# Two projections of a hybrid layer as a 2x2x2 block product with seven instead of eight multiplications

## The chip, the cores and the metric

The kernel runs on one core of one Trainium2 chip. The metric is the device time of one execution in microseconds (us). The engines are named as in the profile: PE (TensorE, matrix products), DVE (VectorE), ACT (ScalarE), POOL (GpSimd) and SP (SyncE, which only issues transfers). SBUF is the on-chip memory, PSUM the accumulators of PE.

## The reference

One layer over 512 tokens of width 1024, all in float32. Only the first part matters here:

```python
proj = rmsnorm(h, norm_mix_g) @ w_in     # (512, 1024) @ (1024, 3592)
fq, fk, fv, ff, gq, gf, gi, gg = split(proj)   # 512, 512, 512, 8, 512, 512, 512, 512 columns
fox_out = fox_attention(fq, fk, fv, log_sigmoid(ff + bias))   # 8 heads of 64
rec = hgrn2_chunkwise(gq, gf, gi, lb)          # 4 heads, state 128x128, gated linear recurrence
rec = rmsnorm(rec, hgrn_norm_g) * silu(gg)
h = h + concat(fox_out, rec) @ w_out
...
```

Cross-attention to 256 memory rows, an MLP of width 4096 with a squared ReLU, and a last RMSNorm follow. `gi` are the recurrence's values, `gg` its output gates: 512 columns each, next to each other in `w_in` (2568 to 3079 and 3080 to 3591).

## The kernel before

Every float32 product is made of three matmuls on numbers of a shorter format: a matrix is split into a high part (`wh...`, by ACT, L179) and the rest (`wl...`, by DVE, L183), and hi x hi, hi x lo and lo x hi are added up in PSUM. The raw weights arrive in tiles `wr...`, loaded by SP (L205); there are two such buffers, so a load waits until the split of the tile two loads earlier has been made. The normalised tokens stand, feature-major, as `hn_hi` and `hn_lo`.

Weights come as panels, listed in `specs`, in two units `a` and `b`; the number in a tile's name is the panel's place in that list. `next_panel` takes the next panel and starts the load and the split of the one after it. Panels 0 to 3 are the recurrence's keys and queries (of `f` and `q`). Panel 4 has the first 256 columns of the values and the 8 forget columns (`proj_if`). Panels 5 and 6 are the gates (`gg`) as two halves of the contraction, 512 columns wide, and panels 7 and 8 the other 256 columns of the values and 256 of the attention's (`gi`): both are `wide` products, made by `gemm_wide` (L281 to L283) in four PSUM tiles, one for each 128 tokens. Panels 9 and up are the attention's.

The products of panels 4 to 8 are not run in one piece. They are generators in the queue `fill`, and the recurrence's preparation takes a budget of them between its own steps, so that PE has work while DVE, ACT and POOL do the elementwise part. That preparation goes through seven levels, m = 1, 2, 4 ... 64: small products `lv` on PE (L800), a masked copy into `Ac` on DVE (L806), multiplications of queries and keys (`sta`, `mov`) by the decays `F` on DVE (L825) and on DVE and POOL (L826), products of decays on POOL (L828), and copies for the next level on ACT (L777, L778). Then come the transposes `pa` of the level result (L878), the transposed keys `pk` (L917) copied to `kt` (L920, for the first block of tokens on DVE), and the scan over four blocks of 128 tokens: outputs `po` (L934), the state product `pst` from `iv` and `kt` (L940), the state, and the gated output `rec` (L961). In the scan, too, matmuls of the queue stand between the blocks.

Two more things have a clock of their own. `COPIES` says how many of the weight copies for the MLP (`wsu`, `wsd`, memory to memory, 512 KB each, issued by SP at L434) follow each weight load from which panel on. `PACE` says at which sum of matmul time and in what steps POOL's accumulating transfers for the MLP are issued.

The tokens' transposes from PSUM also go unscaled into a tile `xT`, from where POOL writes them to memory for later use (`x_park`).

Of the kernel before, what the change touches and what calls it, by code (L numbers as in the profile page):

```python
# [9 lines left out]
F32 = mybir.dt.float32  # L10
# [6 lines left out]
P = 128  # L17
# [21 lines left out]
NEG = -3.0e38  # L39
SEVEN = (1, 2, 3, 4, 5, 6, 7)  # L40
RAWS, HB, LOADS = 5, 4, 8
COPIES = {7: 2, 16: 1, 17: 0, 21: 1}
PACE = (183.0, 4.7), (306.0, 11.5)


@with_exitstack
def emit(
# [58 lines left out]
    def t4(name):  # L106
        return t4p.tile([P, D], F32, tag="t4", name=name)
# [21 lines left out]
    def f(a):  # L129
        return a.bitcast(F32)  # L130
# [58 lines left out]
    def load_unit(name, spec, ks, parts=1, between=None):  # L189

        nw = max(sl.stop for sl, _ in spec)
        uk = ks.stop - ks.start
        hi, lo = new_parts([uk, nw], name)
        state["halves"] += 1
        if len(stream) >= LATE and state["halves"] % 3 == 0:
            raw_ = t4(f"wr{name}")
        else:
            raw_ = wrp.tile([P, uk * nw], F32, tag="wr", name=f"wr{name}", padded_shape=[P, UK * UW])
        raw_ = raw_.rearrange("p (k n) -> p k n", k=uk)
        nk = uk // parts  # L200
        splits = []
        for q in range(parts):
            qs, src_ks = slice(q * nk, (q + 1) * nk), slice(ks.start + q * nk, ks.start + (q + 1) * nk)
            for sl, src in spec:
                nc.sync.dma_start(raw_[:, qs, sl], src[:, src_ks, :])  # L205
            if between is not None:
                between(q)
            for _ in range(next((n for at, n in reversed(COPIES.items()) if len(stream) >= at), 0)):
                if copies:
                    tc.keep_in_program_order(copies.popleft()())  # L210
            splits.append(split_of(hi[:, qs, :], lo[:, qs, :], raw_[:, qs, :]))
        return (hi, lo), splits

    def load_next(parts=2, between=None):

        i = len(stream)
        if i >= len(specs):
            return []
        units, splits = [], []
# [7 lines left out]
        return splits  # L227

    def next_panel():
# [178 lines left out]
    gp.affine_select(out=tri[:, 0, :], in_=tri[:, 0, :], compare_op=ALU.is_ge, fill=0.0, base=0, pattern=[[1, P]], channel_multiplier=-1)  # L408


    hn_hi, hn_lo = act_tile("hn_hi"), act_tile("hn_lo")
    xTd = drp.tile([4, P, 2, S], F32, name="xTd")

# [73 lines left out]
    park = {}  # L487

    ms0 = sm(NT, "ms0")
    gv = cp.tile([P, 33], F32, name="gv")  # L490
# [14 lines left out]
        ve.scalar_tensor_tensor(hn_lo[:, c, :], xps[c], g_mix[:, c : c + 1], f(hn_hi[:, c, :]), op0=ALU.mult, op1=ALU.subtract)  # L505

    def x_park(c):
        part, new_ = c // 2, c // 2 not in park
        if new_:
            park[part] = s4([2, S], f"xT{part}")  # L510
        dst = park[part][:, c % 2, :]
# [4 lines left out]
        if not new_:  # L516
            gp.dma_start(xTd[part], park[part])

    def x_sq(tb):
        junk = s4([D], f"x0j{tb}")  # L520
# [8 lines left out]
    with tc.manual_schedule(engines={mybir.EngineType.Activation, mybir.EngineType.DVE}):  # L529
# [121 lines left out]
    g_x, g_mem, g_ff, g_h = gv[:, 0:8], gv[:, 8:16], gv[:, 16:24], gv[:, 24:25]  # L651
    gate(3)
    forget(3)
    for hp in range(2):
        wt = next_panel()
        for j in range(2):
            h = 2 * hp + j
            ps = mm(f"gq{h}")
            run_now(gemm_fm(ps, wt, j * P, hn_hi, hn_lo))
            ve.tensor_tensor(qt_(h), ps, rbc, ALU.mult)  # L660
            ac.activation(qt_(h), qt_(h), AF.Silu)
# [26 lines left out]
    z = sm(32, "z")  # L688
    z3 = z.rearrange("p (t h) -> p t h", h=FH)

    def proj_if():
        wt = next_panel()
        for tb in range(NT):
            ps = mm(f"gi0{tb}", (WT + FH,))
            yield from gemm_tm(ps, wt, hn_hi, hn_lo, tb)
            ac.activation(iv[tb // 2][:, tb % 2, 0:WT], ps[:, 0:WT], AF.Identity, scale=r0[:, tb : tb + 1])
            ve.scalar_tensor_tensor(z3[:, tb, :], ps[:, WT : WT + FH], r0[:, tb : tb + 1], fb, op0=ALU.mult, op1=ALU.add)
# [6 lines left out]
    fill.add(proj_if(), "ff")  # L704
    fill.add(new(gg, "gg"))
    fill.add(proj_wide([lambda tb: gg[tb // 2][:, tb % 2, :]], AF.Silu, "gg"), "gg")
# [6 lines left out]
    def proj_iv():  # L713
        yield from proj_wide([lambda tb: iv[tb // 2][:, tb % 2, WT:S], new_fv()], AF.Identity, "gi")

    fill.add(proj_iv(), "iv")

# [181 lines left out]
    load_mem(0)  # L899


    mx_hi, mx_lo = act_tile("mx_hi"), act_tile("mx_lo")
    St = None
    pending = None

# [1013 lines left out]
```

## Time and profile before

| | |
|---|---|
| median of 3 runs | 751.66 us (751.61 to 752.14) |
| profiled execution | 751.99 us, of which the span is 750.3 us |
| granted clock of PE, mean | 0.998 of full speed |
| busy: PE, DVE, ACT, POOL | 742.9, 546.5, 444.7, 202.1 us |
| first level product `lv` to first `po` | 65.4 to 125.1 us |

A row of the timeline gives start and duration in us, the engine, the line, the operation, output and inputs by name, the shape, and in brackets how long the engine had been idle before and what ended that. An engine's bracket names the last release only. PE's matmuls overlap, so a matmul's duration is longer than the distance to the next. The stage that the change touches lies between about 25 and 130 us.

### The profile page before, as it was taken

To read this page: it belongs to the slowest core of one execution; us is meant where nothing else is said; L and a number is where in the kernel's file an instruction comes from. 1 tells how busy PE (TensorE), PEld (TensorE's weight loads), DVE (VectorE), ACT (ScalarE), POOL (GpSimd) and SP (SyncE) were. 2 spreads that over 40 slices of the span, in tenths; PEclk is the share of its full clock that TensorE was granted. 3 is DMA by queue.
4 is the path that set the end of the run, shared out by engine and by line. 5 is a ranking of instruction groups with operands and counts; after the bars stand their busy time and mean duration, and the time that the engine had idled before them with its cause. 6 is when DMAs were issued, how large, how long until landed. Compare 5 with 4: busy or idle time off the path is not lost.

```text
span 750.3 us, 12293 instructions
## 1 busy us (share of the span) xinstructions
PE 742.9 (99%) x4581; PEld 649.6 (87%) x4581; DVE 546.5 (73%) x869; ACT 444.7 (59%) x749; POOL 202.1 (27%) x280
## 2 busy tenths in 40 slices
PE   9999999999999999999999999999999999999996
PEld 6889888888888888888888899898989899999985
DVE  5647873667878856645556898978787887878796
ACT  5655555556666742344434589666566757574864
POOL 7207531233433237621111212111111111100034
PEclk9999999999999999999999999999999999999999
DMA  8641987578957889985579799898989898978452
GB/s 250 200 116 58 298 262 228 172 231 269 289 187 224 265 225 210 193 165 122 121 165 197 114 250 238 237 226 247 230 218 235 220 247 214 240 198 232 133 113 113
DMA packets 109678, 152.92 MB, mean 204 GB/s; under 512 B 6145, under 2 KB 76074, under 8 KB 109618
## 3 DMA queue, kind: packets, MB, share of 16 engines
q1 hardware_dynamic: 85458, 112.52, 46.3%
q0 software_dynamic: 24000, 39.35, 30.1%
q8 instruction: 36, 0.59, 0.3%
q14 instruction: 24, 0.20, 0.1%
q10 hardware_dynamic: 160, 0.27, 0.1%
HBM read 147.91 MB, written 51.40 MB: 266 GB/s over the span
## 4 chain that ended last, share of the span: by engine, by line
PE 96%; DVE 1%; issue 1%; ACT 0%; POOL 0%; POOLq 0%; DVEq 0%
PE uU L1494 4%; PE uU L1496 4%; PE uU L1495 4%; PE U L1652 3%; PE U L1653 3%; PE U L1654 3%; PE uY L1495 2%; PE uY L1494 2%; PE uY L1496 2%; PE xk L1008 2%; PE xq L253 2%; PE wo L253 2%; PE xq L254 2%; PE xq L255 2%; PE xw L255 2%; PE xw L254 2%
## 5 line engine op out<-in xcount | busy, mean ns | idle before, releaser
L183 DVE TENSOR_TENSOR wlu<-wru,whu 128x1024 fp32r<-128x1024 f32 x53 | 64.2, 1225 | 28.0 <-ACT whu L179 27.9
L179 ACT ACTIVATE whu<-wru 128x1024 fp32r<-128x1024 f32 x53 | 55.9, 1058 | 43.7 <-PE U L1654 16.8
L183 DVE TENSOR_TENSOR wld<-wrd,whd 128x1024 fp32r<-128x1024 f32 x56 | 68.3, 1222 | 13.5 <-ACT whd L179 13.2
L179 ACT ACTIVATE whd<-wrd 128x1024 fp32r<-128x1024 f32 x56 | 59.0, 1053 | 12.6 <-PE uU L1495 5.2
L1652 PE MATMUL U<-whd,hb 128*128 128x512 f32 x120 | 46.8, 390 | 0.0
L1653 PE MATMUL U<-wld,hb 128*128 128x512 f32 x120 | 46.8, 390 | 0.0
L1654 PE MATMUL U<-whd,hb 128*128 128x512 f32 x120 | 46.7, 389 | 0.0
L1029 POOL TENSOR_SCALAR bi<-nF,Ft 128x128 f32<-128x128 f32 (+3 forms) x32 | 20.6, 652 | 59.8 <-PE pt L1065 38.8
L1494 PE MATMUL uU<-xs_hi,whu 128*128 128x256 f32 x128 | 36.3, 284 | 0.0
L1496 PE MATMUL uU<-xs_hi,wlu 128*128 128x256 f32 x128 | 36.2, 283 | 0.0
L1495 PE MATMUL uY<-xs_lo,whu 128*128 128x256 f32 x128 | 36.2, 283 | 0.0
L1494 PE MATMUL uY<-xs_hi,whu 128*128 128x256 f32 x128 | 36.2, 283 | 0.0
L1496 PE MATMUL uU<-x_hi,wlu 128*128 128x256 f32 x128 | 36.2, 283 | 0.0
L1496 PE MATMUL uY<-xs_hi,wlu 128*128 128x256 f32 x128 | 36.2, 283 | 0.0
L1495 PE MATMUL uU<-xs_lo,whu 128*128 128x256 f32 x128 | 36.2, 283 | 0.0
L1495 PE MATMUL uU<-x_lo,whu 128*128 128x256 f32 x128 | 36.2, 283 | 0.0
L1494 PE MATMUL uU<-x_hi,whu 128*128 128x256 f32 x128 | 36.2, 283 | 0.0
L444 POOL DMA_DIRECT2D wsd<-in_w_dram x16 | 17.9, 1116 | 63.6 <-PE xw L255 12.8
L1390 POOL DMA_DIRECT2D wrd<-in_w_dram x8 | 9.8, 1221 | 86.2 <-DVE wld L183 85.0
L444 POOL DMA_DIRECT2D wsu<-in_w_dram x14 | 17.1, 1218 | 48.9 <-PE xw L255 15.6
L1654 PEld LDWEIGHTS U<-whd,hb 128*128 128x128 f32 x120 | 22.5, 188 | 4.7
L1652 PEld LDWEIGHTS U<-whd,hb 128*128 128x128 f32 x120 | 22.6, 188 | 4.5
(944 smaller groups left out, 2605.2 us busy)
## 6 DMA issues: line engine op xcount, KB each, us to landing
wru<-in_w_dram SPq DMA_DIRECT2D x25, 512.0 KB, 7.9
wsd<-in_w_dram SPq DMA_DIRECT2D x24, 512.0 KB, 7.3
wrd<-in_w_dram SPq DMA_DIRECT2D x24, 512.0 KB, 4.3
wrd<-wsd SPq DMA_DIRECT2D x24, 512.0 KB, 4.9
wsu<-in_w_dram SPq DMA_DIRECT2D x21, 512.0 KB, 5.6
wru<-wsu SPq DMA_DIRECT2D x21, 512.0 KB, 6.1
wsd<-in_w_dram POOLq DMA_DIRECT2D x16, 512.0 KB, 7.8
wsu<-in_w_dram POOLq DMA_DIRECT2D x14, 512.0 KB, 6.9
```

Source lines behind the costliest of these rows:

```text
L179: at = ac.activation(hi, raw, AF.Copy)
L183: at_lo = ve.tensor_tensor(lo, raw, f(hi), ALU.subtract)
L253: te.matmul(ps, wh, hi, start=n_ == 0 and not begun, stop=False)
L254: te.matmul(ps, wh, lo, start=False, stop=False)
L255: at = te.matmul(ps, wl, hi, start=False, stop=k == order[-1])
L444: yield gp.dma_start(wsum[kind, g, name], src, accum_op=ALU.add, **more)
L1494: te.matmul(ps[:, i, :], whi[:, k, ws], xh[:, k, :], start=begin, stop=False, skip_group_check=True)
L1495: te.matmul(ps[:, i, :], whi[:, k, ws], xl[:, k, :], start=False, stop=False, skip_group_check=True)
L1496: at = te.matmul(ps[:, i, :], wlo[:, k, ws], xh[:, k, :], start=False, stop=k == UK - 1, skip_group_check=True)
L1652: te.matmul(ps, hi, whi[:, k, :], start=begin, stop=False, skip_group_check=True)
L1653: te.matmul(ps, hi, wlo[:, k, :], start=False, stop=False, skip_group_check=True)
L1654: at = te.matmul(ps, lo, whi[:, k, :], start=False, stop=k == 1, skip_group_check=True)
```

## The change

Panel 4 now has the attention's 256 columns with the 8 forget columns (`proj_ff`). Values and gates together are a product of 512 tokens x 1024 with 1024 x 1024. Both factors are cut in two by two, tokens into halves of 256, contraction and columns into halves of 512, and the product is made with seven multiplications of sums of blocks instead of eight of blocks (`seven`). Each multiplication is 256 tokens x 512 x 512: 2 x 4 x 3 matmuls 128x512. They run in the order 1, 5, 6, 3, 7, 2, 4, as panels 5 to 11, and accumulate in two pairs of PSUM tiles, `gU` (1, then 6, 7 and 4 on top of it) and `gW` (5, then 3 on top of it; then 2 anew). Products 1 and 4 go to the values through ACT, 5 and 6 to the gates as plain copies on ACT. Products 2, 3 and 7 are added to what is there on DVE (L805, L813), and the gates then get their SiLU on ACT. The panels of the attention move up by three numbers: what was `wr9a` is `wr12a`.

The weight blocks 00, 01, 11 and 10 are loaded once each. 01 and 11 are loaded early, ahead of panel 4's use, into tiles that are free then; 00 goes into the two `wr` buffers; 10 replaces 11 when product 3 has been split. Sums of blocks: 01 + 11 (product 7) on POOL into four tiles, and 00 + 01 (5), that + 11 (6), and that + 10 (4) on DVE in place (L271).

The sums of token blocks are made from the tile `park`, where the unscaled transposes now stay: eight scalings on ACT, four sums on DVE, and their high and low parts on ACT and DVE into the tile `mx`, which is used for something else only later.

`COPIES` moves up with the panel numbers, and eight of the copies that followed the loads of panels 7 and 8 are now issued in two groups of four, right after block 10. `PACE` begins 5 us of matmul time earlier.

```diff
-COPIES = {7: 2, 16: 1, 17: 0, 21: 1}
-PACE = (183.0, 4.7), (306.0, 11.5)
+COPIES = {12: 2, 19: 1, 20: 0, 24: 1}
+PACE = (178.0, 4.7), (301.0, 11.5)
...
-    for n0 in (2056, 2312, 1544, 1800, 2568):
+    for n0 in (2056, 2312, 1544, 1800, 1024):
         specs.append(panel(w_in, n0))
-    specs += wide(w_in, 3080)
-    specs += wide(w_in, 2824, 1024)
+    GORDER = ("1", "5", "6", "3", "7", "2", "4")
...
+    specs += [lambda name=name: product_unit(name) for name in GORDER]
...
+    def early_blocks():
+        load_block("01", "01", [s4p.tile([P, 2, S], F32, tag="s4", name=f"wr01{u}") for u in "ab"])
+        t = t4("wr11b").rearrange("p (k n) -> p k n", k=2)
+        load_block("11", "11", [s4p.tile([P, 2, S], F32, tag="s4", name="wr11a"), t])
+        for k in range(4):
+            t = q2p.tile([P, S], F32, tag="q2", name=f"wr7{k}")
+            a, b = (raw0[n][k // 2][:, k % 2, :] for n in ("01", "11"))
+            gp.tensor_tensor(t, a, b, op=ALU.add)
+            sums7.append(t)
+
+    def product_unit(name):
+        parts = [new_parts([2, S], f"{len(stream)}{u}") for u in "ab"]
...
+            dst, a, b = {"1": (X, X, None), "5": (Y, X, Y), "6": (X, Y, Z), "3": (Z, Z, None), "2": (Z, Z, None), "4": (X, X, Z)}[name]
+            if b is not None:
+                jobs.append(lambda d=dst[u], a=a[u], b=b[u]: ve.tensor_tensor(d, a, b, ALU.add))
+            jobs.append(split_of(hi, lo, dst[u]))
+        if name == "3":
+            jobs.append(lambda: load_block("11", "10", Z))
+        if name in "37":
+            for _ in range(4):
+                jobs.append(lambda: tc.keep_in_program_order(copies.popleft()()))
+        return jobs
...
+        ve.tensor_tensor(hdif["5"], A2b, A2a, ALU.subtract)
+        ve.tensor_tensor(hdif["6"], hdif["5"], A1a, ALU.add)
+        ve.tensor_tensor(hdif["3"], hdif["6"], A1b, ALU.subtract)
+        ve.tensor_tensor(hdif["7"], A1a, A2a, ALU.subtract)
...
+            pss = U if name in "1674" else W
+            whi, wlo = next_panel()
+            xh, xl = hsum[name]
+            for u in range(2):
+                for t, ps in enumerate(pss):
...
+                        at = te.matmul(ps, lo, whi[u][:, kk, :], start=False, stop=end, skip_group_check=True)
+                        yield presum.tick(3 * S / 2400, at)
+                    if u == 1:
+                        done(name, t, ps)
+
+    fill.add(proj_ff(), "ff")
+    fill.add(new(gg, "gg"))
+    fill.add(seven(GORDER[:5]), "gg")
+    fill.add(seven(GORDER[5:]), "iv")
```

Where it moves instructions, three places matter. On PE, ahead of the scan's first block, this stood before; `gi` are products of the last panel of values, `po` and `pst` the scan's first output and state product:

```order
L917 MATMUL pk_1403<-ident,mov_462 128x128
...
L281 MATMUL gi_1170<-wh8b,hn_hi 128x512
L282 MATMUL gi_1170<-wl8b,hn_hi 128x512
L283 MATMUL gi_1170<-wh8b,hn_lo 128x512
L934 MATMUL po_1431<-iv_653,A_1288 128x128 x2
L934 MATMUL po_1431<-iv_653,A_1300 128x128 x2
L940 MATMUL pst_1436<-iv_653,kt_1408 128x128 x4
```

Now, at the same place, with `pq` the attention's first projection (panel 12):

```order
L304 MATMUL pq_1463<-hn_hi,wh12a 128x512
L305 MATMUL pq_1463<-hn_lo,wh12a 128x512
L306 MATMUL pq_1463<-hn_hi,wl12a 128x512
L304 MATMUL pq_1463<-hn_hi,wh12b 128x512
L305 MATMUL pq_1463<-hn_lo,wh12b 128x512
L306 MATMUL pq_1463<-hn_hi,wl12b 128x512
L1057 MATMUL po_1505<-iv_694,A_1355 128x128 x2
L1057 MATMUL po_1505<-iv_694,A_1367 128x128 x2
L1063 MATMUL pst_1510<-iv_694,kt_1497 128x128 x4
```

Between the transposes `pa` and `po` 15 matmuls of the attention's projection now stand, where the last products of the values stood. From the last level to `po` there are 48 matmuls instead of 57.

On DVE, around the copy `kt` that the first `pst` reads, before:

```order
L825 TENSOR_TENSOR mov_462<-mov_462,F_461 128x4x64
L183 TENSOR_TENSOR wl9b<-wr9b,wh9b 128x1024
L183 TENSOR_TENSOR wl10a<-wr10a,wh10a 128x1024
L920 COPY kt_1408<-pk_1403 128x512
L385 TENSOR_TENSOR m0m<-m0m 128x1
```

and now, with `iv` the values to which product 2 is added:

```order
L949 TENSOR_TENSOR mov_460<-mov_460,F_459 128x4x64
L805 SCALAR_TENSOR_TENSOR iv_694<-gW_990,r_432,iv_694 128x512
L805 SCALAR_TENSOR_TENSOR iv_694<-gW_991,r_432,iv_694 128x512
L188 TENSOR_TENSOR wl12a<-wr12a,wh12a 128x1024
L188 TENSOR_TENSOR wl12b<-wr12b,wh12b 128x1024
L188 TENSOR_TENSOR wl13a<-wr13a,wh13a 128x1024
L1043 COPY kt_1497<-pk_1492 128x512
```

Between the last level and `kt` there were two splits; now there are two additions and three splits. What was `wl9a` and stood ahead of the last level is now `wl12a`, behind it.

On SP, the loads of the panels behind the values (`wr`) with the copies (`wsu`, `wsd`), before:

```order
L205 DMA wr9a<-in_w_in_dram 128x4x128 x2
L434 DMA wsu_200<-in_w_dram 512x1x256
L434 DMA wsd_203<-in_w_dram 256x1x512
L205 DMA wr9b<-in_w_in_dram 128x4x128 x2
L434 DMA wsu_201<-in_w_dram 512x1x256
L434 DMA wsd_204<-in_w_dram 256x1x512
L205 DMA wr10a<-in_w_in_dram 128x4x128 x2
```

and now, from block 10 on:

```order
L243 DMA wr11a<-in_w_in_dram 128x2x512
L243 DMA wr11b<-in_w_in_dram 128x2x512
L487 DMA wsu_194<-in_w_dram 512x1x256
...
L487 DMA wsd_203<-in_w_dram 256x1x512
L210 DMA wr12a<-in_w_in_dram 128x4x128 x2
L487 DMA wsu_201<-in_w_dram 512x1x256
L487 DMA wsd_204<-in_w_dram 256x1x512
L210 DMA wr12b<-in_w_in_dram 128x4x128 x2
L487 DMA wsu_202<-in_w_dram 512x1x256
L487 DMA wsd_205<-in_w_dram 256x1x512
L210 DMA wr13a<-in_w_in_dram 128x4x128 x2
```

Eight copies stand together ahead of `wr12a`; from there on the row is as it was.

More of the change, by code (lines that the diff above doesn't have):

```diff
@@ L218, in load_next @@
             return []
+        if callable(specs[i]):
+            return specs[i]()
         units, splits = [], []
@@ L486, in emit @@
     presum.jobs.extend(j for _, j in sets)
-    park = {}
     ms0 = sm(NT, "ms0")
@@ L507, in x_park @@
     def x_park(c):
[L508 to L511, printed above, removed]
+        part, dst = c // 2, park[:, c, :]
         if c % 2 == 0:
@@ L515, in x_park @@
             ve.tensor_copy(dst, xps[c])
-        if not new_:
-            gp.dma_start(xTd[part], park[part])
+        parked.add(c)
+        if c ^ 1 in parked:
+            gp.dma_start(xTd[part], park[:, 2 * part : 2 * part + 2, :])
     def x_sq(tb):
@@ L689, in emit, with proj_ff @@
     z3 = z.rearrange("p (t h) -> p t h", h=FH)
-    def proj_if():
+    def proj_ff():
         wt = next_panel()
+        dst = new_fv()
         for tb in range(NT):
@@ L702, in new @@
         yield
-    fill.add(proj_if(), "ff")
-    fill.add(new(gg, "gg"))
-    fill.add(proj_wide([lambda tb: gg[tb // 2][:, tb % 2, :]], AF.Silu, "gg"), "gg")
     def new_fv():
@@ L711, in new_fv, with seven, tok, done @@
         return lambda tb, n0=0: t[:, tb, :]
-    def proj_iv():
-        yield from proj_wide([lambda tb: iv[tb // 2][:, tb % 2, WT:S], new_fv()], AF.Identity, "gi")
-    fill.add(proj_iv(), "iv")
+    U, W = [], []
+    def seven(names):
+        def tok(ts, tb):
+            return ts[tb // 2][:, tb % 2, :]
+        def done(name, t, ps):
+            if name == "1":
+                ac.activation(tok(iv, t), ps, AF.Identity, scale=r0[:, t : t + 1])
+            elif name == "2":
+                ve.scalar_tensor_tensor(tok(iv, t), ps, r0[:, t : t + 1], tok(iv, t), op0=ALU.mult, op1=ALU.add)
+            elif name == "4":
+                ac.activation(tok(iv, 2 + t), ps, AF.Identity, scale=r0[:, 2 + t : 3 + t])
+            elif name in "56":
+                ac.activation(tok(gg, t + (2 if name == "5" else 0)), ps, AF.Copy)
+            else:
+                tb = t + (2 if name == "7" else 0)
+                g_ = tok(gg, tb)
+                ve.tensor_tensor(g_, ps, g_, ALU.add)
+                ac.activation(g_, g_, AF.Silu, scale=nr0[:, tb : tb + 1])
+        for name in names:
+            if name == "1":
+                U.extend(mm(f"gU{t}") for t in range(2))
+            elif name == "5":
+                W.extend((mm("gW0"), pvt("gW1")))
+            pss = U if name in "1674" else W
+            whi, wlo = next_panel()
+            xh, xl = hsum[name]
+            for u in range(2):
+                for t, ps in enumerate(pss):
+                    ts_ = slice(t * P, (t + 1) * P)
+                    for kk in range(2):
+                        k = 2 * u + kk
+                        hi, lo, begin, end = xh[:, k, ts_], xl[:, k, ts_], name in "125" and k == 0, k == 3
+                        te.matmul(ps, hi, whi[u][:, kk, :], start=begin, stop=False, skip_group_check=True)
+                        te.matmul(ps, hi, wlo[u][:, kk, :], start=False, stop=False, skip_group_check=True)
+                        at = te.matmul(ps, lo, whi[u][:, kk, :], start=False, stop=end, skip_group_check=True)
[6 more added lines that the diff above has]
+    fill.add(seven(GORDER[5:]), "iv")
     Ac = []
```

54 lines of the change are left out of this document (51 added, 3 removed).

## The prediction

> **What bounds the kernel now.** The page comes first: the engines' busy shares, and the chain of work that ended last.
>
> ```profile
> PE 742.9 (99%) x4581; PEld 649.6 (87%) x4581; DVE 546.5 (73%) x869; ACT 444.7 (59%) x749; POOL 202.1 (27%) x280
> ...
> PE 96%; DVE 1%; issue 1%; ACT 0%; POOL 0%; POOLq 0%; DVEq 0%
> ```
>
> TensorE (PE) is never idle for long, and 96% of the chain is its own work. A matmul taken away is worth its full price, as long as nothing makes PE wait for its operands. So I need the price of a matmul, and who is near to being late in the stage that changes, which the windows show:
>
> ```profile
> 77.33 0.39 PE L282 MATMUL gg<-wl5a,hn_hi 128*128 128x512 f32 x1
> ...
> 78.47 0.39 PE L281 MATMUL gg<-wh5b,hn_hi 128*128 128x512 f32 x1
> ```
> ```profile
> 20.00:40.00 20.00, 20.00 (x93) 16.38 (x92) 13.72 (x23) 14.00 (x22) 3.98 (x6) 1.00 0.57 178
> 40.00:60.00 20.00, 20.00 (x129) 16.97 (x128) 9.68 (x11) 9.33 (x12) 3.51 (x2) 1.00 0.50 135
> 60.00:80.00 20.00, 20.00 (x202) 17.60 (x203) 15.70 (x33) 12.28 (x27) 12.94 (x14) 1.00 0.31 95
> 80.00:100.00 20.00, 20.00 (x168) 16.39 (x169) 14.52 (x37) 11.91 (x23) 10.33 (x14) 1.00 0.93 303
> 100.00:120.00 20.00, 20.00 (x133) 16.94 (x132) 11.64 (x22) 7.99 (x12) 4.89 (x10) 1.00 0.80 245
> ```
>
> Five matmuls after 77.33 the next one starts at 78.47, so one costs 0.228 us of PE, though each is shown 0.39 long. In the windows the columns are the stretch, its length, then busy time of PE, PEld, DVE, ACT and POOL, the granted clock (1.00: nothing to gain there) and the DMA share. DVE (VectorE) has 4.3, 5.5 and 8.4 us free in the three stretches from 60 to 120: these 18.2 us are the room for what the change adds.
>
> **The change part by part.** *The matmuls.* Values and gates took 2 x 4 x 8 x 3 = 192 matmuls 128x512; seven products of 2 x 4 x 3 are 168. 24 x 0.228 = 5.47 us less PE. Nothing is added on PE. This is the whole gain, and the rest is what PE has to wait.
>
> *The early part.* Eight scalings, four token sums and their parts fall at 30 to 55 us, where DVE and ACT are each idle 6 us of one stretch of 20 and 10 of the next. GpSimd's four sums of block pairs stand ahead of its first row below, whose bracket is the idle time before it: four at 1.28 are 5.1 us in 26.59. If that cover were gone, the multiply behind them and the levels would come 5.1 later. I cost all this at nothing; below that it cannot go, since work is only added, and above I allow one sum that finds no gap, 1.2.
>
> ```profile
> 56.45 1.28 POOL L734 TENSOR_TENSOR mov<-mov,F 128x512 f32<-128x512 f32 x1 [26.59 <-PE dg L730]
> 57.69 2.28 POOL L734 TENSOR_TENSOR sta<-sta,F 128x512 f32<-128x512 f32 x1
> ```
> ```profile
> 55.71 0.69 DVE L660 TENSOR_TENSOR sta<-gq,rbc 128x512 f32<-128x512 f32 x1 [0.63 <-PE gq L255]
> 56.41 0.42 DVE L733 TENSOR_TENSOR Ac<-dg,id 128x256 f32<-128x256 f32 x1
> 56.93 1.88 DVE L183 TENSOR_TENSOR wl5b<-wr5b,wh5b 128x1024 fp32r<-128x1024 f32 x1
> ...
> 73.09 1.23 DVE L183 TENSOR_TENSOR wl6a<-wr6a,wh6a 128x1024 fp32r<-128x1024 f32 x1 [1.43 <-ACT wh6a L179]
> 74.24 0.22 DVE L697 SCALAR_TENSOR_TENSOR z<-gi,r,fb 128x8 f32<-128x8 f32 x1
> ...
> 80.26 0.37 DVE L752 TENSOR_TENSOR pre<-pre,lf 128x8 f32<-128x8 f32 x2
> 81.35 1.23 DVE L183 TENSOR_TENSOR wl7a<-wr7a,wh7a 128x1024 fp32r<-128x1024 f32 x1 [0.72 <-ACT wh7a L179]
> ...
> 101.31 0.19 DVE L758 COPY Ft<-pF 128x32 f32<-128x32 f32 x1
> ...
> 109.20 0.68 DVE L765 COPY Fr<-pFr 8x512 f32<-8x512 f32 x1 [1.53 <-PE pFr L763]
> ```
>
> *Who is late.* With 24 fewer matmuls the recurrence's levels stay at their places in PE's order, but what follows them comes 24 matmuls sooner. In the new order 15 matmuls of the next projection stand ahead of the first state product `pst`, and 9 are simply gone. `pst` needs `kt`, a copy on DVE, which in the new order stands behind `wl13a`, the low half of a weight split. Before, the rows there were these:
>
> ```profile
> 126.02 1.06 PE L940 MATMUL pst<-iv,kt 128*128 128x128 f32 x8
> ```
> ```profile
> 119.58 1.23 DVE L183 TENSOR_TENSOR wl10a<-wr10a,wh10a 128x1024 fp32r<-128x1024 f32 x1 [4.21 <-ACT wh10a L179]
> 121.87 0.69 DVE L920 COPY kt<-pk 128x512 f32<-128x512 f32 x1 [1.07 <-PE pk L917]
> ```
> ```profile
> 118.49 1.06 ACT L179 ACTIVATE wh10a<-wr10a 128x1024 fp32r<-128x1024 f32 x1 [4.38 <-PE gi L283]
> ```
>
> So `kt` was ready at 122.6, 3.4 ahead of `pst` at 126.02. After the change PE comes to `pst` 9 x 0.228 = 2.05 sooner, at 123.97. When is `kt` done? I walk along DVE's new order from the second level (copies of m=2) to `wl12a`. The DVE busy time of the stretch ahead of it and of the six levels, with the stretch's length first:
>
> ```profile
> 59.20:76.04 16.84, 11.73 (x22) 1.00 0.14 39
> 76.04:79.85 3.81, 3.81 (x12) 1.00 0.97 317
> 82.50:86.18 3.68, 3.68 (x11) 1.00 1.08 372
> 89.18:92.40 3.22, 3.22 (x11) 1.00 0.73 221
> 95.00:98.40 3.40, 3.20 (x11) 1.00 0.83 251
> 101.90:105.30 3.40, 3.23 (x10) 1.00 0.83 220
> 110.10:113.70 3.60, 3.41 (x6) 1.00 1.03 328
> ```
>
> - Start: a split costs 1.15 from start to start (73.09 to 74.24). A sum of two blocks is the same shape with two SBUF inputs; no row shows one, so I take the split's 1.15 (below it, 0.70, the add of half the size at 55.71 to 56.41; above it, 1.88, `wl5b`). Four sums and one moved split add 5.75 ahead of the level, against 5.11 of idle time (16.84 - 11.73). If all of it is used the level is 0.6 late, if the 1.43 before `wl6a` stays, 2.0 late. I take the middle: 76.04 + 1.35 = 77.4.
> - Six levels: 3.81 + 3.68 + 3.22 + 3.20 + 3.23 + 3.41 = 20.55.
> - Eleven splits, `wl7a` to `wl12a`: 11 x 1.15 = 12.65. Two block sums: 2.3.
> - Six evacuations of PSUM that add (products 3, 7 and 2): 6 x 0.70 = 4.2.
> - The small ones: 0.19 and 0.68 in the rows above, the pair at 80.26 with 0.37, and two more like it just ahead, 0.36: 1.6.
> - Waits for ACT's high halves: now 0.7 to 1.4 for a split, but the new order has other work ahead of most. I take one, the 0.72 before `wl7a`.
>
> 77.4 + 20.55 + 12.65 + 2.3 + 4.2 + 1.6 + 0.7 = 119.4 at the end of `wl12a`. The low half is needed by the third matmul behind the transposes `pa`, which stand where they stood:
>
> ```profile
> 119.18 0.39 PE L283 MATMUL gi<-wh8b,hn_lo 128*128 128x512 f32 x1
> ```
>
> So PE waits 0.2 there, which is part of the longer wait that follows.
>
> Now the load of `wr13a` starts: its buffer is that of `wr12a`, free only when `wl12a` has been made. Price of issue and landing from the loads before:
>
> ```profile
> 107.71 0.93 SPq L205 DMA_DIRECT2D wr10a<-in_w_in_dram x2
> ```
> ```profile
> wr7b<-in_w_in_dram SPq DMA_DIRECT2D x2, 256.0 KB, 6.2
> ...
> wr9b<-in_w_in_dram SPq DMA_DIRECT2D x2, 256.0 KB, 2.9
> ...
> wr10b<-in_w_in_dram SPq DMA_DIRECT2D x2, 256.0 KB, 4.0
> ```
>
> The last number is us from issue to landing. I take 4.0, the row nearest in time and in what is queued (2.9 below, 6.2 above, when copies are ahead). 119.4 + 0.93 + 4.0 = 124.33; the high half on ACT 1.06 gives 125.39; `wl13a` 1.23, 126.62; `kt` 0.69, 127.31. PE waits 127.31 - 123.97 = 3.34 us there, and 5.47 - 3.34 = 2.1 us are left of the gain. Behind `pst` the scan's products stand 15, 12 and 15 matmuls apart (before 15, 12, 30), all 2.7 us or more, as two of the three gaps were before, so I cost the rest at nothing.
>
> In SP's queue eight weight copies that were spread over four panels now stand together ahead of `wr12a`. With a DMA share of 0.80 to 0.93 in these stretches they are the reason not to take the 2.9.
>
> Against the profiled run's own 751.99 (span 750.3, 1.7 around it) that is 749.9; from the median 751.66 it is 749.6. A run of this kernel can be told from no change beyond about 0.2%, 1.5 us.
>
> **The rivals.**
>
> *A, nothing waits.* If `kt` is there by 123.97, the whole 5.47 remains: 746.2. It needs 3.3 off the walk: landing 2.9 gives 1.1, no wait for ACT 0.7, a start at 76.6 gives 0.8, evacuations hidden in other waits the rest. For it: 18.2 us of DVE idle in the stage. Against: all must happen. Chance 0.13.
>
> *B, the gain is eaten.* The load of `wr13a` lands like `wr7b`, 6.2 after its issue, because copies stand ahead of it. Then `kt` comes at 129.5, PE waits 5.5, and the 5.47 are gone: 751.7. For it: the DMA share is 0.80 to 0.93 in these stretches. Another landing between and small waits at the levels give the same. Chance 0.22.
>
> *C, slower: DVE and GpSimd hold each other up.* `wl5b` took 1.88 beside GpSimd's multiply, 0.65 over the 1.23 of a split alone, and that multiply 2.28, 1.0 over the one before. In the new order 13 such instructions with two SBUF inputs (eleven splits, two sums) stand back to back among GpSimd's multiplies, while before they stood in their own gaps. Each that meets one costs 0.65, and DVE has little left to take it up: all of it arrives at `kt`. From 6 of 13 on (3.9 us against the 2.1 gained) it is slower by over 0.2%; with 8 it is 8 x 0.65 - 2.1 = +3.1, 754.8; with 10, +4.4, 756.1. GpSimd being late itself delays the level products on PE, for which I have no row. For it: GpSimd is busy 10.33 of 20 us at 80 to 100. Against: some of the levels' rows hold such meetings already. The Trainium skill speaks against this change here: "SBUF — State Buffer", "Who interferes with whom", says that a DVE instruction with two SBUF inputs contends with a GpSimd instruction that reads SBUF, and that the loser is blocked for the whole instruction. The two rows agree in kind; 0.65 is less than the 1.28 of the multiply, and by a full block each the price of ten would be 12.8 instead of 6.5, which would make it 762.4. Chance of C 0.30.
>
> **How the numbers follow.** The forecast, PE waiting about 3.3 us for `kt`, has 0.35, its own range 747.9 to 751.0: landing 2.9 or DVE 1.1 ahead gives -1.1 more, the level 0.7 earlier -0.6; an ACT wait more and the level 0.7 later +1.4. Faster by over 0.2%: A 0.13, the forecast but for its upper end 0.31, a little of B 0.04: 0.48. Same: 0.04 + 0.18 = 0.22. Slower: 0.30. The range must hold 8 in 10: down to A's 746.2, rounded 746.0, and up to C with ten meetings, 756.1, rounded 756.0; that leaves out C beyond ten, and a little below A.
>
> **What would show it.** Right: PE idle in one block of about 3 us ahead of `pst`, released by DVE `kt`; ACT's high half of panel 13 waiting for its DMA; SP's issue of `wr13a` waiting for DVE `wl12a`; PE without idle time at 60 to 118. B: the same, with over 6 us to landing. A: no idle PE there. C: splits and sums of 1.6 to 2.3 instead of 1.23, and PE idle ahead of the level products `lv` as well. Wrong in another way: PE waiting before 60 for the token parts, or for PSUM handed between products, or for the early blocks on SP; or PE idle behind the scan.

## The result, and the profile after

The changed kernel takes 758.78 us (758.27 to 759.41, 4 runs) against 751.66: ratio 1.0094, 95% interval 1.0076 to 1.0111. It is 7.1 us slower, where 2.1 faster was forecast. The profiled execution took 758.7 us, its span is 757.0 (before 750.3).

The page, busy shares and the chain that ended last:

```profile
PE 740.2 (98%) x4557; PEld 646.2 (85%) x4557; DVE 578.1 (76%) x898; ACT 459.3 (61%) x769; POOL 209.5 (28%) x284
...
PE 85%; DVE 6%; ACT 4%; issue 2%; POOL 1%; DMA 1%; POOLq 0%; DVEq 0%; SPq 0%; ACTq 0%
```

PE has 24 matmuls less, as meant. But the chain, which was 96% PE, is now 85% PE with 12% of VectorE, ScalarE, GpSimd and transfers in it: somebody keeps PE waiting. Whom PE waited for (sum in us, times, longest); in the kernel before this list held only the first 1.3 us of the program, the `warm` row:

```profile
PE pst L1063 <- DVE kt L1043: 2.6, 1, 2.6
PE lv L924 <- DVE mov L949: 1.9, 3, 1.0
PE pk L1040 <- ACT A L1003: 1.8, 1, 1.8
PE warm L416 <- DVE ones L420: 1.3, 1, 1.3
PE lv L924 <- DVE Ac L857: 1.2, 1, 1.2
PE pt L1188 <- DVE dn L1175: 0.8, 1, 0.8
PE pq L306 <- DVE wl12a L188: 0.7, 1, 0.7
```

The windows put these in their places; the columns are those of the prediction's windows:

```profile
60.00:80.00 20.00, 18.75 (x193) 16.70 (x190) 20.00 (x30) 10.50 (x22) 9.90 (x8) 1.00 0.01 2
80.00:100.00 20.00, 18.54 (x160) 14.70 (x159) 19.33 (x39) 12.78 (x24) 11.50 (x18) 1.00 0.29 85
100.00:120.00 20.00, 19.39 (x125) 16.30 (x124) 19.57 (x39) 16.18 (x26) 5.83 (x10) 1.00 0.75 241
120.00:140.00 20.00, 14.83 (x73) 11.96 (x72) 10.57 (x18) 8.04 (x20) 2.91 (x7) 0.91 1.06 357
```

Three things are to be seen. VectorE is busy 20.00, 19.33 and 19.57 of 20 us: of the 18.2 us that it had free from 60 to 120, 1.1 are left. The transfers, at a share of 0.01 from 60 to 80, crowd at 1.06 behind 120. And PE is idle for 1.25 + 1.46 + 0.61 + 5.17 = 8.5 us, and its clock falls to 0.91 in the last window. The rows around `kt` on VectorE, and on ScalarE ahead of it:

```profile
79.42 0.72 DVE L930 COPY_PREDICATED Ac<-mku,lv 128x128 f32<-128x128 uint8 x2
...
122.50 1.22 DVE L188 TENSOR_TENSOR wl12a<-wr12a,wh12a 128x1024 fp32r<-128x1024 f32 x1
126.28 1.22 DVE L188 TENSOR_TENSOR wl12b<-wr12b,wh12b 128x1024 fp32r<-128x1024 f32 x1 [2.56 <-ACT wh12b L184]
131.60 1.23 DVE L188 TENSOR_TENSOR wl13a<-wr13a,wh13a 128x1024 fp32r<-128x1024 f32 x1 [4.10 <-ACT wh13a L184]
132.75 0.68 DVE L1043 COPY kt<-pk 128x512 f32<-128x512 f32 x1
```
```profile
125.19 1.06 ACT L184 ACTIVATE wh12b<-wr12b 128x1024 fp32r<-128x1024 f32 x1 [5.26 <-DMA wr12b<-in_w_in_dram]
126.15 1.25 ACT L807 ACTIVATE iv<-gU,r 128x512 f32<-128x512 f32 x2
127.29 1.08 ACT L1003 ACTIVATE A<-pa 128x512 f32<-128x512 f32 x2
130.51 1.06 ACT L184 ACTIVATE wh13a<-wr13a 128x1024 fp32r<-128x1024 f32 x1 [2.14 <-DMA wr13a<-in_w_in_dram]
```

ScalarE stands 5.26 us before the high half of 12b, whose load is not there, and the copies `A`, which need nothing but the transposes `pa` that PE made at 122.0 and 124.1, stand behind it. VectorE stands 4.10 before `wl13a`, with `kt` behind it. On PE:

```profile
133.49 1.32 PE L1063 MATMUL pst<-iv,kt 128*128 128x128 f32 x8 [2.62 <-DVE kt L1043]
...
135.32 0.78 PE L304 MATMUL pq<-hn_hi,wh12b 128*128 128x512 f32 x1
...
137.60 0.48 PE L306 MATMUL pq<-hn_hi,wl12b 128*128 128x512 f32 x1
```
```profile
132.00:134.00 2.00, 0.51 (x4) 1.00 1.12 362
134.00:136.00 2.00, 2.00 (x12) 0.59 1.07 398
136.00:138.00 2.00, 2.00 (x7) 0.56 1.11 357
138.00:140.00 2.00, 2.00 (x11) 1.00 1.04 370
```

After the wait the clock is granted at 0.59 and 0.56 for some 4 us (the last column but two; these windows show PE alone). From `pst` to the sixth `pq` matmul behind it takes 137.60 - 133.49 = 4.11 us, where before it took 126.02 to 128.51, 2.49: 1.6 us more.

Put together for the span: -5.5 for the matmuls, +8.5 idle, +1.6 slow clock, +0.8 for a wait at `pt` in the attention, which the kernel before does not have (no run here shows why; in the experiments on the changed kernel it is 0.2 to 1.8). That is +5.4 of the measured +6.7. The rest lies in the waits themselves. Idle time counts from the end of a matmul's row, which is shown 0.39 long, though without a wait the next one would start 0.23 after it:

```profile
125.70 0.40 PE L306 MATMUL pq<-hn_hi,wl12a 128*128 128x512 f32 x1
127.94 0.33 PE L1040 MATMUL pk<-ident,sta 128*128 128x128 f32 x1 [1.84 <-ACT A L1003]
```

From start to start this wait is 127.94 - 125.70 - 0.23 = 2.0, not 1.84. Counted so, against the same pairs of rows in the kernel before, the waits from 65 to 134 are 10.0 instead of 8.5, and the sum is +6.9.

### The profile page after: what moved, and what is told of

Same layout as the page of the kernel before. It is cut to its first block, busy times and chain, and to the rows that moved or that the text cites. A ratio compares the mean times of both kernels' runs of the same rounds, so it can differ in the third digit from the quotient of the medians.

```text
span 757.0 us, 12292 instructions
## 1 busy us (share of the span) xinstructions
PE 740.2 (98%) x4557; PEld 646.2 (85%) x4557; DVE 578.1 (76%) x898; ACT 459.3 (61%) x769; POOL 209.5 (28%) x284
## 4 chain that ended last, share of the span: by engine, by line
PE 85%; DVE 6%; ACT 4%; issue 2%; POOL 1%; DMA 1%; POOLq 0%; DVEq 0%; SPq 0%; ACTq 0%
PE uU L1617 4%; PE uU L1619 4%; PE uU L1618 4%; PE U L1775 4%; PE U L1776 4%; PE U L1777 4%; PE uY L1619 2%; PE uY L1617 2%; PE uY L1618 2%; PE xk L1131 2%; PE xq L304 2%; PE wo L304 2%; PE xq L305 2%; PE xq L306 2%; PE xw L304 2%
```

## The experiments

Two theories stood at first. **V**: VectorE is full from 60 to 122, and everything that it feeds is late. **L**: the loads of panels 12 and 13 come too late and among too many copies. Later came **H** (not the load, but what stands behind a waiting split in an engine's row, is what costs) and, once V stood, the question whether VectorE is full by its own work alone (bare length; the expectations call it theory B, which is not the prediction's rival B) or because GpSimd stretches it (theory C, the prediction's slower rival). Some kernels leave a part of the computation out; the text says which, and they are no versions to be used.

All ratios are to the kernel before; what is called better or slower in us is against the changed kernel's 758.78 unless said otherwise.

### Loads, copies, and what stands behind them

```diff
 e1_copies_early
-COPIES = {12: 2, 19: 1, 20: 0, 24: 1}
+COPIES = {14: 2, 19: 1, 20: 0, 24: 1}
-        if name in "37":
-            for _ in range(4):
+        if name in "156":
+            for _ in range({"1": 8}.get(name, 4)):
```

> All 16 weight copies that stood behind block 10 and behind the loads of panels 12 and 13 are issued right behind block 00, at about 57 us, where the transfer engines of the changed kernel are idle until 92. Nothing on VectorE changes. Theory L (late loads: the loads of panels 12 and 13 are crowded by copies, and ScalarE stands waiting for them): the second unit of panel 12 lands 4 us after its issue instead of 7, PE's waits at pk (1.8) and much of that at the first pst (2.6) and the slow clock behind it (about 1.8) go, some 4 to 5 us: 754. Theory V (VectorE is full from 60 to 122, and that alone sets the time): at most 1 us: 758.

757.04 us, ratio 1.0073 (1.0056 to 1.0091): 1.7 better. 12b lands sooner, ScalarE waits 1.4 for it instead of 5.3, but then stands 4.5 before `wh13a`, with the second `A` behind it, and PE waits 1.3 at `po` and 0.9 at `pst`. L holds a part, not the whole.

```diff
 e2_panel12_early
+        elif name == "12a":
+            raw_ = raw0["01"][0].rearrange("p k n -> p (k n)")
```

> The first unit of panel 12 is loaded into a tile that block 01 leaves free, so it can be loaded at about 80 us instead of waiting for wl11a, and each following unit (12b, 13a) gets its buffer one split earlier; the copies stay where they are. Theory L: wl12b and wl13a come some 5 us sooner, PE's waits at pk and pst and the slow clock go: about 753. Theory V: PE is still 3.7 us late at pa and kt stands behind the same splits: at most 1 us, 758.

760.97, 1.0128 (1.0113 to 1.0144): slower, against both theories. The scheduler put the split of 13a ahead of the copies `A` as soon as its buffer was free; ScalarE stood 4.5 us before `wh13a` and 3.7 before `wh13b`, and PE waited 4.2 at `pst`. An earlier buffer brought the next split's wait for its load forward.

e3_both has both edits.

> Both edits together: copies early and the first unit of panel 12 early. Theory L: nothing is left of the waits at pk and pst, what stays are the 3.7 us that PE is late at pa, less the 5.5 of the removed matmuls: 750 to 752. Theory V: 757 to 758.

761.24, 1.0125 (1.0110 to 1.0140): again slower, against both. Now `wh13b` stands ahead of the second `A` and waits 7.6 for its load; PE waits 4.3 at `po`. With loads alone at most e1's 1.7 is mended: this led to H.

```diff
 e5_behind     (put_behind: the split of that unit comes later on the engine than the given instruction)
-        ac.activation(Ag[hp][:, 4:8, :], pa, AF.Copy)
+        at = ac.activation(Ag[hp][:, 4:8, :], pa, AF.Copy)
+        for key in KEYS:
+            put_behind(key, at)
...
-            ve.tensor_copy(kts[c], pk)
+            at = ve.tensor_copy(kts[c], pk)
+            for key in KEYS[-2:]:
+                put_behind(key, at)
```

`KEYS` is `('12b', '13a', '13b')`; the splits of 13a and 13b go behind the copy of the first state, too.

> Only the order changes: the splits of 12b and of panel 13 are put behind ScalarE's copies of the transposes pa and behind VectorE's kt (and panel 13's behind the copy of the first state), so that a split that waits for its load keeps nothing else waiting. Loads, copies and sums as in the changed kernel. Theory H (the load itself costs nothing; the row of instructions behind the waiting split does): the waits at pk (1.8) and pst (2.6) and the slow clock (about 1.8) go but for 1 us: 753 to 754. Theory V (VectorE full): the late copies were late because of VectorE before them, and the same time is lost a little later: 757 to 758.

760.14, 1.0106 (1.0089 to 1.0123): no gain at all. The first `pst` did come at 130.59 with no wait. The wait came back one block later; ScalarE, then PE of this run:

```profile
136.56 1.06 ACT L203 ACTIVATE wh13b<-wr13b 128x1024 fp32r<-128x1024 f32 x1 [2.83 <-DMA wr13b<-in_w_in_dram]
137.53 0.26 ACT L1105 ACTIVATE hj<-po 128x128 f32<-128x128 f32 x1
```
```profile
141.34 2.04 PE L1086 MATMUL pst<-iv,kt 128*128 128x128 f32 x8 [4.04 <-DVE rec L1109]
```

The squares `hj` of the scan's first output stood behind `wh13b`, the output `rec` behind them, and with it the PSUM tile of the second `pst`. H alone falls as well: with loads this late, something else stood behind them.

e6_behind_copies has this order and e1's early copies.

> The order edit together with the early copies. Theory H: the loads no longer matter, so nothing or at most 1 us over the order edit alone: 752.5 to 753.5. Theory L (late loads): 1.5 us or more over the order edit alone. Theory V: 757.

754.98, 1.0038 (1.0023 to 1.0053): 3.8 better than the change, where the two edits alone gave 1.7 and nothing. Together they give more than the two apart. What PE still waits is 3.9 at `lv`, 0.7 at `pq`, 0.8 at the second `pst` and 1.2 at `pt`: VectorE in every one.

### Less work for VectorE

```diff
 e4_no_sums    (products 5, 6 and 4 use one block)
-            if b is not None:
+            if b is not None and False:
```

> The six sums of weight blocks on VectorE are left out (products 5, 6 and 4 use one block instead of a sum), copies and loads as in the changed kernel. 6 x 1.2 = 7.3 us less on VectorE. Theory V: the levels are no longer late (3.1 us of PE waits at lv go), wl12a is done 5 to 7 us sooner, and the waits at pk and pst and the slow clock go too: 750 to 751. Theory L: the levels' waits go, but the loads of 12b and 13a still land 6 to 7 us after their issue behind the copies, and PE still waits 2 to 4 us there: 753 to 755.

753.50, 1.0029 (1.0019 to 1.0039): 5.3 better, between the two. VectorE has 6 sums less, 7.3 us by the expectation; `wl12a` ends at 118.7 instead of 123.7 and PE waits 0.3 at `lv`; but 12b still holds ScalarE for 4.5 us, and 3.4 of waits at `pk`, `po` and `pst` stay, with a clock of 0.91. V and L each hold a part.

e7_behind_no_sums adds the order edit to it.

> The order edit and no sums of weight blocks on VectorE (products 5, 6 and 4 use one block). If H and V each own a part and they add up: the 3 us of waits at the levels and the 3.4 us of waits at pk, po and pst with the slow clock behind them are all gone, and the 5.5 us of removed matmuls remain but for 2: 748 to 749. If the removed matmuls were not worth their price at all, it stays at 752 or more.

754.68, 1.0039 (1.0026 to 1.0052): no better than e4, and 6 us above the parts added up. PE waits 4.1 at the second `pst`, as in e5_behind. That is where the expectation had the removed matmuls worth less than their price; the next run speaks against that.

e9_all_three has no sums, the order edit and the early copies.

> Order edit, early copies and no sums of weight blocks on VectorE (products 5, 6 and 4 use one block) in one kernel. If the loss is the sum of three parts (VectorE late at the levels; loads of panels 12 and 13 crowded by copies; instructions that stand behind a waiting split), none is left here, and the removed matmuls show: 5.5 less than before but for about 1 us at the end of the attention: 747 to 748. If there is a fourth cost that no run has taken away: 750 or more.

750.09, 0.9977 (0.9968 to 0.9986). With all three taken away the removed matmuls show at last: 1.6 faster than before, with 1.0 and 0.3 left at `lv`, 0.9 at `pst`, 0.8 at `pt`. 5.5 less these 3.0 is 2.5; the other 0.9 were not looked for. The expectation was 2 us better, and had 750 or more as the sign of a fourth cost: these waits are what none of the three edits takes away.

### GpSimd beside VectorE

```diff
 e13_after_no_pool_levels
-                (ve, gp)[j].tensor_tensor(kv[:, :, 0, :], kv[:, :, 0, :], ...)
-            gp.tensor_tensor(fv[:, :, 0, 0:1], fv[:, :, 0, 0:1], ...)
+                if j == 0:
+                    ve.tensor_tensor(kv[:, :, 0, :], kv[:, :, 0, :], ...)
```

> The changed kernel, with GpSimd's part of the levels left out (its multiply of keys by the decay and its products of decays, L950 second half and L952); VectorE's row of instructions stays. It tells how much of VectorE's lateness is its own longer work and how much is GpSimd beside it. Theory C (contention): durations of VectorE's splits, sums and level multiplies fall to 1.2 and 0.4 us each, 12 us shorter in all, kt comes 4 us sooner or more, 752 to 755. Theory B (bare length): VectorE's added sums and evacuations alone fill its time, and GpSimd's part was hidden: at most 1.5 us, 757 or more.

750.43, 0.9982 (0.9972 to 0.9991): 8.3 better with no sum or load touched, and `kt` still behind `wl13a`; theory C had asked for 4 to 7. `wl12a` ends at 117.2 instead of 123.7. Its control, the same lines out of the kernel before:

> The kernel before with the same part left out, as the control for the other run of this call. PE has no waits there to lose, so by both theories it stays within 0.5 us: 751 to 752. If it falls by 1 us or more, the other run's gain counts only beyond that.

751.40, 0.9996 (0.9987 to 1.0005): unchanged. The groups of VectorE's level multiplies from 57 to 122 (count, busy us, mean ns), of the kernel before, of the changed one and of e13:

```profile
L825 DVE TENSOR_TENSOR mov<-mov,F 128x256 f32<-128x256 f32 x14 | 8.2, 586 | 0.1
L825 DVE TENSOR_TENSOR sta<-sta,F 128x256 f32<-128x256 f32 x14 | 7.7, 550 | 0.0
L826 DVE TENSOR_TENSOR sta<-sta,F 128x256 f32<-128x256 f32 x14 | 7.6, 546 | 1.3 <-POOL F L828 1.1
```
```profile
L949 DVE TENSOR_TENSOR sta<-sta,F 128x256 f32<-128x256 f32 x14 | 10.5, 748 | 0.0
L950 DVE TENSOR_TENSOR sta<-sta,F 128x256 f32<-128x256 f32 x14 | 7.9, 563 | 0.0
L949 DVE TENSOR_TENSOR mov<-mov,F 128x256 f32<-128x256 f32 x14 | 7.3, 523 | 0.1
```
```profile
L949 DVE TENSOR_TENSOR mov<-mov,F 128x256 f32<-128x256 f32 x14 | 6.1, 436 | 0.1
L949 DVE TENSOR_TENSOR sta<-sta,F 128x256 f32<-128x256 f32 x14 | 5.9, 419 | 0.0
L951 DVE TENSOR_TENSOR sta<-sta,F 128x256 f32<-128x256 f32 x14 | 5.9, 419 | 0.0
```

The same 42 multiplies take 23.5 us before, 25.7 after, and 17.9 where GpSimd's part of the levels is left out. So 5.6 us of stretching were there before, at no cost, because VectorE had time (e14 takes 4.2 of them away, 23.5 to 19.3, and gains nothing); the change adds 2.2 and takes that time away. With that of splits and sums (under the reasons below) the stretching is the part that VectorE could not carry. e13 also takes away GpSimd as a supplier of `F` and `mov`; VectorE is not seen waiting for these in the changed kernel's levels, so what it measures is mostly the stretching, but it isn't that alone.

```diff
 e17_mul_on_dve
-                (ve, gp)[j].tensor_tensor(kv[:, :, 0, :], ...)
+                ve.tensor_tensor(kv[:, :, 0, :], ...)
```

> The changed kernel with the whole computation; only GpSimd's multiply of keys in each level (L950, two instructions) goes to VectorE, 14 instructions of some 0.34 us, 4.8 us more of work there. GpSimd keeps the products of decays. If the price of meeting GpSimd is what fills VectorE (about 9 us of stretching in all): VectorE still ends 2 to 4 us sooner, 754 to 757. If moving work only moves time: 759 or more.

755.26, 1.0047 (1.0034 to 1.0060): the whole computation, 5.8 us *more* instructions on VectorE, and 3.5 us faster. `wl12a` ends at 121.1 instead of 123.7: the multiplies cost VectorE less than meeting them did, and bare length as the only cause falls. It is a part of the cause all the same: e4, with six sums less and GpSimd's work as it was, gained 5.3, and in the kernel before the same stretching cost nothing. VectorE is overfull by the added work and the stretching together, and taking either away gives back most of it. (Of the 3.5 us 2.6 are the earlier `wl12a`; the other 0.9 may come from the order: with these durations the scheduler put `kt` ahead of `wl13a` here.) PE's longest wait is now this one, and its clock falls behind it, to 0.50 from 126 to 128: the matmuls stand 0.42 apart instead of 0.23.

```profile
125.56 0.46 PE L1040 MATMUL pk<-ident,sta 128*128 128x128 f32 x1 [2.03 <-ACT A L1003]
...
126.89 0.63 PE L305 MATMUL pq<-hn_lo,wh12a 128*128 128x512 f32 x1
127.31 0.63 PE L306 MATMUL pq<-hn_hi,wl12a 128*128 128x512 f32 x1
```

e15_e6_mul_on_dve adds the order edit and the early copies.

> The same multiplies on VectorE, together with the order edit and the early copies (that pair took 755.0). If stretching by GpSimd is the larger part: 751 to 753; else 755 or more.

750.90, 0.9991 (0.9982 to 1.0000), 11 runs of 750.64 to 751.68: together with e16 below, the best version with the whole computation. It equals the kernel before, or beats it by 0.1%. All that PE still waits for in it:

```profile
PE lv L943 <- DVE Ac L876: 1.7, 1, 1.7
PE warm L435 <- DVE ones L439: 1.3, 1, 1.3
PE pst L1086 <- DVE rec L1109: 0.8, 1, 0.8
PE pt L1213 <- DVE dn L1200: 0.6, 1, 0.6
```

### Sums by accumulating transfers

```diff
 e8_dma_sums   (with e5's order; the order of products becomes 1, 5, 3, 6, 7, 2, 4)
+            dst, more = {"1": (X, None), "5": (Y, "00"), "6": (Y, "11"), "3": (Z, None), "2": (Z, None), "4": (Y, "10")}[name]
...
-                jobs.append(lambda d=dst[u], a=a[u], b=b[u]: ve.tensor_tensor(d, a, b, ALU.add))
+                jobs.append(lambda d=dst[u], u=u: gp.dma_start(d, block0(more)[:, 2 * u : 2 * u + 2, :], accum_op=ALU.add))
```

> A version meant to be used, with the whole computation: the order edit, and the sums for products 5, 6 and 4 made by accumulating transfers from memory into the block's tile instead of by VectorE, with product 3 ahead of 6 to give the transfer time. VectorE loses the six sums, GpSimd issues six transfers more (about 1 us each). If what holds is VectorE: like the run without sums, 748 to 750. If GpSimd's issues among the levels delay its multiplies: PE waits at lv again, 752 to 754.

758.07, 1.0082 (1.0067 to 1.0097), missed. PE waited 5.4 us at `gW` for ScalarE's copy of product 5, since product 3 now follows it at once in the same PSUM tile.

e10_dma_sums2 keeps the products' order, with 8 copies behind panel 12's load (`COPIES = {12: 4, 13: 0, 14: 2, ...}`).

> The whole computation: the order edit; the sums for products 5, 6 and 4 by accumulating transfers, with the products in their first order 1, 5, 6, 3, so that product 3 doesn't wait for the copy of product 5; block 00's buffers are free early, so panel 12 is loaded at about 66 us with eight copies right behind it, none behind panel 13. If the causes add up and the transfers land in time (some 8 us after their issue): 748 to 750. If GpSimd, waiting for a split before it issues an accumulating transfer, holds up its multiplies of the levels: PE waits at lv for 2 to 4 us, 751 to 754.

759.13 (757.01 to 762.04), 1.0098 (1.0080 to 1.0117), missed. GpSimd stood 4.0 us before each of two of these transfers, waiting for VectorE, with a level's multiplies behind it, and ScalarE 4.3 for a transfer to land; PE waited 3.8 at `lv` and its clock was 0.84 from 80 to 100.

e11_four_sums_off (order edit and early copies; product 5's sums by transfers, 6's on VectorE, 4's on GpSimd):

> The whole computation, with the order edit and the early copies: the sums for product 5 by accumulating transfers issued before the levels begin, those for product 4 on GpSimd, only those for product 6 left on VectorE and put behind the level's multiplies. If VectorE's length is what is left of the loss (the run with order edit and early copies took 755.0 with six sums on VectorE, 750.1 with none): about a third of the way from the better end, 751 to 752.5. If GpSimd's additions (4 x 1.3 us and more beside VectorE) hold up its own multiplies: 753 to 754.5.

759.86, 1.0101 (1.0087 to 1.0116), missed: GpSimd waited 3.5 us for block 10 in the middle of the levels, PE 3.3 at `gU`, at a clock of 0.74 from 100 to 120.

e12_four_sums_dma (4's sums by transfers too):

> As the other run of this call, but the sums for product 4 too by accumulating transfers, which GpSimd issues when product 6 has been split. GpSimd has less to do, but stands waiting for that split ahead of the multiplies of a level. If that wait is short: 750.5 to 752. If it holds up the level: PE waits 1 to 3 us more at lv, 752.5 to 755.

754.29, 1.0042 (1.0027 to 1.0057), with a wide spread (12 runs of 752.20 to 757.25): about e6's time, and the worse of the two cases expected. PE still waits 1.7 and 1.0 in two of the levels.

e16_e12_mul_on_dve has e17's edit besides.

> The same multiplies on VectorE, together with the order edit, the early copies and the sums for products 5 and 4 by accumulating transfers. GpSimd's multiplies no longer stand behind its wait for the split of product 6. If stretching and that wait were what was left: 749.5 to 751.5, a version that beats the kernel before or equals it; else 752 to 754.

751.07 (750.39 to 754.60), 0.9991 (0.9982 to 1.0000): the same as e15, where none of the sums is moved. With GpSimd's multiplies gone, moving the sums off VectorE gains nothing more.

## Why the prediction was wrong

**The matmuls.** Right: 24 fewer at 0.228. In e9 a part of their gain appears, 1.6 us, with 3.0 of idle time left.

**The place.** Right: `pst` waits for `kt`, `kt` stands behind `wl13a`, `wl13a` waits for a load that waits for `wl12a`. `kt` was forecast for 127.31 and ended at 133.43. The 6.1 us are these terms:

- *The start, 77.4 by the sum.* The level of m=2 began at 79.42: 2.0 later, and later than the 78.0 that the sum had as its worst case. The early part ahead of it, at 30 to 55 us, did cost next to nothing: the `Ac` that stood at 56.41 before starts at 56.56. But the block sums and the split between them did not find VectorE alone. Rows of the changed kernel, the first three ahead of that level:

```profile
60.78 2.31 DVE L271 TENSOR_TENSOR wr01b<-wr00b,wr01b 128x1024 f32<-128x1024 f32 x1
63.02 2.31 DVE L188 TENSOR_TENSOR wl5b<-wr00b,wh5b 128x1024 fp32r<-128x1024 f32 x1
...
68.05 1.88 DVE L271 TENSOR_TENSOR wr00a<-wr01a,wr11a 128x1024 f32<-128x1024 f32 x1
...
90.04 1.68 DVE L188 TENSOR_TENSOR wl8a<-wr11a,wh8a 128x1024 fp32r<-128x1024 f32 x1
```

- *The walk to `wl12a`, 42.0 by the sum.* It took 79.42 to 123.72, 44.3: 2.3 more. The levels took 21.9 instead of 20.55, the eleven splits 13.75 instead of 12.65, waits 0.5 more; the additions and small ones 0.6 less. The step that failed, here and at the start, is the one that took the durations of levels, splits and sums from rows of the trace before as if they belonged to the instructions: they are durations beside an idle gap here and a busy GpSimd there, and when splits and sums fill the gaps, more instructions meet GpSimd.
- *The load, 0.93 + 4.0.* This term was mis-sized. From `wl12a` to `wh13a` 6.8 us went by, 1.9 more; the landing was 5.9, at the upper row (6.2), not the middle one. Rival B had the price right.

**PE at the levels, costed at nothing.** PE waited 3.1 us there. VectorE, which sets `kt`, does not wait for PE in the levels, so without these waits PE would have stood as much longer at `pst`: they add nothing to the 6.1. But they were not seen; nor was ScalarE's row, where 12b's wait held up `A` and `iv` before `kt` was even asked for.

**Behind `pst`.** Costed at nothing; 1.6 for the slow clock and 0.8 at `pt`. So -2.1 + 6.1 + 1.6 + 0.8 = +6.4, of 6.7 between the two profiled executions.

**The rivals.** C had the mechanism, the sign and the place, and was given 0.30. Its price was one-sided. It counted the 13 splits and sums from `wl7a` to `wl12a`: only two of these, `wl8a` at 1.68 and `wl10a` at 1.52, met GpSimd by more than 0.3 us, 0.8 together, where its examples had 8 and 10 at 0.65. Three more, in the rows above, stood ahead of them, where it did not look, and it held the level multiplies to be paid already, where 2.2 were added. And it stopped there: a late VectorE releases buffers late, which makes loads late, which ended in PE's clock. B and C did not exclude each other, as the list of chances took them to; both happened, and the range's upper end, C alone at ten meetings, was too low by 2.8.

The rule of the Trainium skill that was weighed there ("SBUF — State Buffer", "Who interferes with whom": two SBUF inputs on VectorE against a GpSimd instruction that reads SBUF) agrees with e13, e14 and e17 in kind. The 762.4 worked out from a full block at each of ten meetings did not come: the largest stretch of a split or sum was 1.1 (2.31 against 1.22), and only five of the twenty from 58 to 118 were stretched by 0.3 or more. In two rows the stretch is no longer than what was left of GpSimd's instruction at their start: `wr01b` starts at 60.78, a multiply on GpSimd ends at 62.01 (1.2 left, 1.09 longer), and `wl8a` starts at 90.04, a product of decays ends at 90.64 (0.6 left, 0.46 longer).

## What to carry to other kernels

Free time on an engine is priced by rows in which its neighbours may be idle: here VectorE was busy for 70% of the time from 60 to 120, went to 98%, and paid for meeting its neighbour. So price an engine's instructions by the slowest row beside that neighbour, and ask whether moving the neighbour's work *onto* it is cheaper (e17: 5.8 us more work, 3.5 us less time). Where a split waits for a load, look at what stands behind it on its engine's row, in every engine that the split uses; mending the order alone gave nothing here and the early copies alone 1.7 us, since the wait moved on, and the two together gave 3.8. And when a bound is taken away, price the chain as a whole, late buffers and all, instead of one wait at its end.

## What the runs showed of the hardware

The clock of PE fell to half behind some waits, and the length of the wait does not tell which. In the changed kernel it stayed at 1.00 behind a wait of 1.84 us and was granted at 0.59 and 0.56 for about 4 us behind the next, of 2.62, with 2.9 us of work between them. In e1 it fell after two of 1.33 and 0.89, one close behind the other (0.91 over that window of 20 us), in e17 after a single one of 2.03, with nothing over 0.1 in the 50 us ahead of it (the rows are shown with e17). Waits of 0.8 to 1.8 us that stood alone, in e9, e13 and e15, left it at 1.00, and so did one of 2.07 in e10:

```profile
143.09 1.13 PE L1086 MATMUL pst<-iv,kt 128*128 128x128 f32 x8 [2.07 <-DVE rec L1109]
```
```profile
140.00:160.00 20.00, 17.93 (x117) 1.00 0.83 268
```

The Trainium skill, "TensorE: Matmul & The Clock Gate", "Part 1: The HAM clock gate", puts the fall behind an idle window of some 3.4 us; the 2.03 of e17 and the 2.62 of the changed kernel are shorter, so here the traces do not agree with it. What decides between 2.03 and 2.07 no run here shows.

Multiplies of 128x256 on VectorE took 0.40 us at their shortest and up to 1.6 beside GpSimd, a 128x1024 split or sum 1.22 and up to 2.31. In the kernel before this stretching was 5.6 us of VectorE's level work by the rows of e13, and taking 4.2 of it away (e14) changed nothing: a cost of this kind stays unseen in the time until the engine has no room left.
